# Moving eight modulation chunks within the RWKV stage of a two-block transformer kernel

## The chip, the cores and the metric

The kernel runs on one core of one Trainium2 chip. The metric is the device time of one execution in microseconds (us); for the kernel before it is the median of 3 runs.

## What is computed

Two transformer blocks on one sequence of 512 tokens of width 1024, in float32. The change lies in the first block, which mixes a dilated attention and an RWKV-7 recurrence, gated, and modulates its normalized inputs and its residuals by six vectors worked out from a conditioning vector `c`:

```python
ada = (c @ w_ada[l] + b_ada[l])[:, None, :]
sh1, sc1, gt1, sh2, sc2, gt2 = jnp.split(ada, 6, axis=-1)
h = rms_norm(x, norm1_w[l]) * (1.0 + sc1) + sh1
proj = h @ w_in[l]
att_in, rwkv_in, gate_in = jnp.split(proj, [ATT_IN, ATT_IN + RWKV_IN], axis=-1)
y_att = attention_mixer(att_in) @ w_att_out[l]
y_rwkv = rwkv7_mixer(rwkv_in, ...) @ w_rwkv_out[l]
g_att, g_rwkv = jnp.split(jax.nn.sigmoid(gate_in + b_gate[l]), N_BRANCHES, axis=-1)
x = x + gt1 * ((g_att * y_att + g_rwkv * y_rwkv) @ w_o[l])
h = rms_norm(x, norm2_w[l]) * (1.0 + sc2) + sh2
x = x + gt2 * conv_ffn(h, w_up[l], conv_w[l], conv_b[l], w_down[l])
```

`rwkv7_mixer` shifts its projections by one token, makes r, k and v from them and runs a state recurrence over the tokens for 16 heads. The second block (two attentions and a mixture of 32 experts) is not touched.

## The kernel before

**Products.** A float32 product is made of three fp32r ones. `raw_load` (line 216) fetches 1 MB of weights into one of two buffers tagged `raw`. `split` (225) copies them to `hi` on ACT and writes the rest, `lo`, on GpSimd and DVE in turn; each half of a raw buffer is the weights of one 128-row output tile, and there are four `hi`/`lo` pairs. `dense` (250) then runs 24 matmuls of 128x128 on 128x512 into a PSUM bank tagged `mm`, of which there are two (`MM`, 179). A raw buffer comes free when both halves are split.

**The modulation.** w_ada is read in 24 chunks of 256 columns, 1 MB each. The first 8 (sh1, sc1) are done before the first norm, and those from 16 on later, on DVE. Chunks 8 to 15 (gt1, sh2) are the generator `ada_group` (281), called for two groups of four: one step for each chunk (its load into a `raw` buffer, 8 matmuls with a 32-column stationary operand, 16 in the trace since float32 goes in two passes, into an `mm` bank, and a DVE copy or add into `rows`), and a fifth step that finishes a group (two transposes into an `mm` bank, a DVE reduction and an add). Chunks are not split; their `raw` buffer comes free when TensorE has read it. The results are first used behind the RWKV and attention stages.

**The RWKV stage** goes through four quarters of four heads (`rwkv_quarter`, 599). A quarter makes, for each of two tiles `i2`, the decay, then k, r and v in this order (s = 1, 0, 2; each a `dense` product whose bank `shift`, 509, empties with one instruction on ACT and one on DVE), then the small matmuls of the chunked recurrence, which it masks into `SA` and `SB` and sends through DRAM (`Ad`). Then DVE inverts 64 triangular 32x32 blocks in 31 steps (`Ti`, lines 721 to 729), the result goes through DRAM once more (`Td`) and comes back to two groups of 32x32 matmuls (`px`, `py`), and the recurrence runs over 8 chunks of 64 tokens, with three groups of small matmuls (`SA`, `TT`, `SB`) and copies in each. At its end the output is normalized per head.

**Fillers.** Beside this runs `fw`, a chain of the attention's q and k products (`f_qk`), its v products (`f_v`, 128x256 matmuls, three weight loads for each half) and the gates (`f_gate`), cut in steps. A quarter has a budget of 4 x nw steps; it pulls 28 of them at points of its recurrence, and `run_fill` (821) emits what is left behind the quarter. In the second and third quarters `run_fill` also takes five steps of `fa`, the chain of the two `ada_group`s, in turn with the fillers.

**Order.** The program is written through a tile framework: emission gives each instruction its rank, and a planner that knows what waits for what puts instructions on the engines' queues, by rank among those that it holds to be ready; buffers are handed out the same way. An engine then runs its queue in order. All weight loads and all stores go through SP's queue.

Of the kernel before, what the change touches and what calls it, by code (L numbers as in the profile page):

```python
# [161 lines left out]
def body(tc, I, O):  # L162
# [4 lines left out]
    with es:  # L167
# [8 lines left out]
        def G(tag="a"):  # L176
            return pp.tile([128, 512], F32, tag=tag, bufs=3, name=tag)

        def MM():
            return pp.tile([128, 512], F32, tag="mm", bufs=2, name="mm")  # L180

        def mm(out, l, r, start=True, stop=True):
            return nc.tensor.matmul(out, l, r, start=start, stop=stop, skip_group_check=True)  # L183
# [7 lines left out]
        def V(n, j=None, w=1):  # L191
            o, m = PVO[n]
            return pv[:, o:o + m] if j is None else pv[:, o + j:o + j + w]
# [52 lines left out]
        def pull(g, n):  # L246
            for _ in islice(g, n):
                pass

        def dense(acc, w, xs, late=False):  # L250
            hi, lo = w
            n = len(xs)
            for k, (xh, xl) in enumerate(xs):
                mm(acc, hi[:, k], xh, start=(k == 0), stop=False)
                mm(acc, hi[:, k], xl, start=False, stop=False)
                if not late:
                    mm(acc, lo[:, k], xh, start=False, stop=(k == n - 1))
            for k, (xh, _) in enumerate(xs if late else ()):
                mm(acc, lo[:, k], xh, start=False, stop=(k == n - 1))
# [21 lines left out]
        def ada_group(chs, pool=None, bufs=RAWB):  # L281


            rows = adp.tile([128, 256], F32, tag="rows", bufs=1, name="rows")
            for m, ch in enumerate(chs):
                raw = raw_load(I['wada'][ch], pool, bufs).rearrange("p (k c) -> p k c", k=8)
                acc = MM()
                for k in range(8):
                    j = k % 4
                    mm(acc[32 * j:32 * j + 32, 0:256], c32[:, k, 3 - m:35 - m], raw[:, k], start=(k < 4), stop=(k >= 4))  # L290
                if m == 0:
                    nc.vector.tensor_copy(rows, acc[:, 0:256])
                else:
                    nc.vector.tensor_add(rows, acc[:, 0:256], rows)
                yield
            n = len(chs)
            acc = MM()
            for s in range(2):
                nc.tensor.transpose(acc[:, 128 * s:128 * s + 128], rows[:, 128 * s:128 * s + 128], ident)
            o = 2 * chs[0]  # L300
            a = ada[0][:, o:o + 2 * n]
            nc.vector.tensor_reduce(a.rearrange("p (m s) -> p m s", s=2), acc[:, 0:256].rearrange("p (s j m) -> p m s j", s=2, j=4)[:, :n], axis=mybir.AxisListType.X, op=OP.add)
            nc.vector.tensor_add(a, a, V('bada', o, 2 * n))
            yield
# [204 lines left out]
        def shift(acc, m, mu, om, dst):  # L509
            nc.scalar.activation(dst[:m], acc[:m], AF.Copy, scale=om[:m])  # L510
            nc.vector.scalar_tensor_tensor(dst[:m, 1:512], acc[:m, 0:511], mu[:m], dst[:m, 1:512], op0=OP.mult, op1=OP.add)
# [36 lines left out]
        def f_qk(hg):  # L548
            for ch in range(6):
                gr, s = ch // 2, ch % 2  # L550
                for t, w in enumerate(wstream(I['wqk'][6 * hg + ch], 8)):
                    acc = MM()
                    yield from dense_g(acc, w, H)
                    o = rp.tile([128, 512], F32, tag="stg", bufs=2, name="stg")
                    if s == 0:
                        ov = o.rearrange("p (b r i) -> p b r i", b=4, r=4)
                        nc.scalar.activation(ov, acc.rearrange("p (b i r) -> p b r i", b=4, r=4), AF.Copy, scale=-0.125)
                    elif gr == 0:
                        nc.scalar.copy(o, acc)
                    else:  # L560
                        nc.scalar.copy(o.rearrange("p (r j) -> p r j", r=4), acc.rearrange("p (j r) -> p r j", r=4))
                    nc.sync.dma_start(qk_d[12 * hg + 4 * gr + 2 * s + t], o)
                    yield
# [25 lines left out]
        def f_gate(j0, j1):  # L589
            for j in range(j0, j1):  # L590
                for t, w in enumerate(wstream(I['wg'][j], 8)):
                    acc = MM()
                    yield from dense_g(acc, w, H)
                    o = gpool[0].tile([128, 512], F32, tag="stg", bufs=2, name="stg")
                    nc.scalar.activation(o, acc, AF.Tanh, scale=0.5, bias=bgh[:, 8 * t + j:8 * t + j + 1])
                    nc.sync.dma_start(gt_d[2 * j + t], o)
                    yield

        def rwkv_quarter(q, fw):
            T = lambda shape, tag, bufs=1, dt=F32: (rpa if tag in EARLY else rp).tile(list(shape), dt, tag=tag, bufs=bufs, name=tag)  # L600
            w2q = T([65, 256], "w2q")
            nc.sync.dma_start(w2q, I['w2a'][:, 256 * q:256 * q + 256])
# [15 lines left out]
            for i2 in range(2):  # L618
# [16 lines left out]
                for s in (1, 0, 2):  # L635
                    if early_rkv:
                        acc = early_rkv.pop(0)
                    else:
                        acc = MM()
                        dense(acc, next(rkv_it), H)  # L640
                    d = T([128, 512], "rkv"[s], 2 if s < 2 else 1)
                    shift(acc, 128, V('mu', 8 * s + i), omu[:, 8 * s + i:8 * s + i + 1], d)
                    z[s] = d
                    if s == 1:
                        ksq = T([128, 512], "tmp", 2)
                        nc.scalar.activation(ksq, d, AF.Square, scale=V('kk', i))
                        km2 = T([128, 512], "km2")
                        nc.scalar.activation(km2, ta, AF.Identity, scale=V('ka', i), bias=ka2[:, i:i + 1])
                        nc.gpsimd.tensor_mul(km2, km2, d)
                        BKf = T([128, 8, 2, 64], "BKf")  # L650
                        nc.gpsimd.tensor_mul(BKf[:, :, 1], c8(km2), Dh)
                    elif s == 0:
                        sps = G()
                        for t in range(4):
                            mm(sps[:, 2 * t:2 * t + 2], ksq[:, 128 * t:128 * t + 128], hs2)
                        rn = T([128, 8], "rn")
                        nc.vector.tensor_scalar(rn, sps[:, 0:8], 1e-24, None, op0=OP.max)
                        nc.scalar.activation(rn, rn, AF.Sqrt)
                        nc.vector.reciprocal(rn, rn)
                        AR = T([128, 8, 2, 64], "AR", 2)  # L660
                        nc.gpsimd.tensor_mul(AR[:, :, 1], c8(d), Dp)
                        prod = T([128, 512], "tmp", 2)
                        nc.vector.scalar_tensor_tensor(prod, d, rkh[:, i:i + 1], km2, op0=OP.mult, op1=OP.mult)
# [157 lines left out]
        def run_fill(*gens):  # L821
            gens = list(gens)
            while gens:
                for g in list(gens):
                    try:
                        next(g)
                    except StopIteration:
                        gens.remove(g)

        fa = chain(*[ada_group(range(o, o + 4)) for o in range(8, 16, 4)])  # L830
        fw = chain(f_qk(0), f_v(0), f_qk(1), f_v(1), f_gate(0, 8))
        for q, (nw, na) in enumerate(((11, 0), (14, 5), (14, 5), (10, 0))):
            fq = islice(fw, 4 * nw)
            rwkv_quarter(q, fq)
            run_fill(fq, islice(fa, na))
        ra_.close()

        yas = ExitStack()
# [162 lines left out]
        fa = ada_cols(fp, [(0, 16, 4)], after, lag=0)  # L1001
# [35 lines left out]
        fa = ada_cols(fp, [(0, 20, 4), (1, 0, 24)], [h2i])  # L1037
# [486 lines left out]
        m2, i2, oh2 = first_max(e2, 8, "y")  # L1524
# [100 lines left out]
        q = R([128, 4], "q")  # L1625
# [216 lines left out]
```

## Time and profile before

| | |
|---|---|
| median of 3 runs | 2034.93 us (2030.18 to 2035.95) |
| the profiled execution | 2040.78 us, span 2039.0 us |
| TensorE matmul busy | 1932.9 us (95%) |
| DVE, ACT, GpSimd busy | 1146.4, 728.3, 436.8 us |
| mean granted TensorE clock | 0.966 of full speed |
| last stores of the four RWKV quarters (`yrw_d`) | issued at 229, 374, 559 and 736 us |

The profile is of one execution. Its times are in microseconds from the span's start. PE is TensorE, POOL is GpSimd; PEclk is the granted TensorE clock as a share of full speed, which is 2.4 GHz, and 0.50 is 1.2 GHz. A busy TensorE is one with matmuls in it; at half clock the same matmuls take twice as long and count as busy all the time.

### The profile page before, as it was taken

To read this page: it belongs to the slowest core of one execution; us is meant where nothing else is said; L and a number is where in the kernel's file an instruction comes from. 1 tells how busy PE (TensorE), PEld (TensorE's weight loads), DVE (VectorE), ACT (ScalarE), POOL (GpSimd) and SP (SyncE) were. 2 spreads that over 40 slices of the span, in tenths; PEclk is the share of its full clock that TensorE was granted. 3 is DMA by queue.
4 is the path that set the end of the run, shared out by engine and by line. 5 is a ranking of instruction groups with operands and counts; after the bars stand their busy time and mean duration, and the time that the engine had idled before them with its cause. 6 is when DMAs were issued, how large, how long until landed. Compare 5 with 4: busy or idle time off the path is not lost. (4 is left out here: it accounts for less than half of the span.)

```text
span 2039.0 us, 28480 instructions
## 1 busy us (share of the span) xinstructions
PE 1932.9 (95%) x11085; PEld 1442.3 (71%) x11085; DVE 1146.4 (56%) x2232; ACT 728.3 (36%) x1261; POOL 436.8 (21%) x273
## 2 busy tenths in 40 slices
PE   7999999999999899999999989999999999599997
PEld 4788787787888767777887767777779667444553
DVE  4573573463437354557898873174430562467776
ACT  3533423342343243324333332354332452322222
POOL 1421311220232111131322322221111131122221
PEclk9999999997999999999999999999999899799998
DMA  7233244324234254244655544222233341699994
GB/s 298 78 105 104 80 120 146 117 95 122 92 104 166 81 199 163 95 166 145 199 194 181 181 160 147 92 90 82 89 114 104 98 181 40 241 421 424 424 423 195
DMA packets 100048, 334.11 MB, mean 164 GB/s; under 512 B 30212, under 2 KB 35080, under 8 KB 76360
## 3 DMA queue, kind: packets, MB, share of 16 engines
q1 hardware_dynamic: 97608, 323.89, 44.7%
q0 software_dynamic: 2304, 8.39, 1.1%
q8 instruction: 88, 1.44, 0.3%
q14 instruction: 48, 0.39, 0.1%
HBM read 304.98 MB, written 27.26 MB: 163 GB/s over the span
## 5 line engine op out<-in xcount | busy, mean ns | idle before, releaser
L231 POOL TENSOR_TENSOR lo<-raw,hi 128x1024 fp32r<-128x1024 f32 (+1 forms) x108 | 261.1, 2417 | 904.9 <-ACT hi L228 803.3
L228 ACT CAST hi<-raw 128x1024 fp32r<-128x1024 f32 (+1 forms) x215 | 222.3, 1038 | 368.5 <-PE mm L183 303.0
L183 PE MATMUL mm<-hl,hi 128*128 128x512 f32 x1008 | 333.3, 405 | 0.3 <-ACT stv L584 0.3
L183 PE MATMUL mm<-h,hi 128*128 128x512 f32 x784 | 248.3, 396 | 8.1 <-DVE u L1054 6.0
L231 DVE TENSOR_TENSOR lo<-raw,hi 128x1024 fp32r<-128x1024 f32 (+1 forms) x107 | 140.5, 1313 | 197.9 <-ACT hi L228 196.6
L183 PEld LDWEIGHTS mm<-hl,hi 128*128 128x128 f32 x1008 | 189.6, 191 | 42.1 <-issue 6.3
L183 PE MATMUL mm<-hl,lo 128*128 128x512 f32 x504 | 202.1, 401 | 0.0
L183 PEld LDWEIGHTS mm<-h,hi 128*128 128x128 f32 x784 | 146.5, 189 | 45.4 <-issue 12.3
L356 DVE SCALAR_TENSOR_TENSOR asum<-araw,cv,asum 128x256 f32<-128x256 f32 x224 | 151.5, 680 | 25.7 <-DMA araw<-in_wada 20.7
L183 PE MATMUL mm<-h,lo 128*128 128x512 f32 x392 | 153.9, 393 | 0.0
L183 PE MATMUL mm<-fm,hi 128*128 128x512 f32 x352 | 111.4, 397 | 6.1 <-ACT fm L1058 6.1
L183 PE MATMUL b<-h,hi 128*128 128x512 f32 x368 | 115.8, 392 | 0.0
L183 PE MATMUL mm<-gu,XT 128*64 128x512 f32 x512 | 113.2, 595 | 0.0
L183 PEld LDWEIGHTS mm<-hl,lo 128*128 128x128 f32 x504 | 96.0, 190 | 20.3 <-issue 2.2
L183 PEld LDWEIGHTS mm<-gu,XT 128*64 128x64 f32 x512 | 36.8, 138 | 73.0 <-issue 63.5
L183 PEld LDWEIGHTS mm<-h,lo 128*128 128x128 f32 x392 | 74.2, 189 | 15.8 <-issue 0.2
L183 PEld LDWEIGHTS mm<-fm,hi 128*128 128x128 f32 x352 | 66.7, 191 | 22.1 <-ACT fm L1058 6.5
L183 PEld LDWEIGHTS b<-h,hi 128*128 128x128 f32 x368 | 69.7, 190 | 14.7 <-issue 0.2
L183 PE MATMUL b<-h,lo 128*128 128x512 f32 x184 | 72.2, 392 | 0.0
L183 PE MATMUL mm<-fm,lo 128*128 128x512 f32 x176 | 69.2, 393 | 0.0
L893 ACT ACTIVATE sc<-sc,st 128x512 f32<-128x512 f32 (+3 forms) x96 | 56.3, 588 | 26.6 <-DVE st L891 22.3
L183 PE MATMUL mm<-hi,hl 128*128 128x256 f32 x384 | 57.6, 296 | 2.8 <-ACT stv L584 2.8
(522 smaller groups left out, 3554.1 us busy)
## 6 DMA issues: line engine op xcount, KB each, us to landing
gu<-in_wgu SPq DMA_DIRECT2D x32, 2048.0 KB, 15.0
araw<-in_wada SPq DMA_DIRECT2D x128, 256.0 KB, 3.3
dn<-in_wde SPq DMA_DIRECT2D x32, 1024.0 KB, 14.8
raw<-in_wup SPq DMA_DIRECT2D x22, 1024.0 KB, 4.8
raw<-in_wada SPq DMA_DIRECT2D x16, 1024.0 KB, 5.9
raw<-in_wg SPq DMA_DIRECT2D x16, 1024.0 KB, 5.0
raw<-in_wrkv SPq DMA_DIRECT2D x12, 1024.0 KB, 5.1
raw<-in_wqk SPq DMA_DIRECT2D x12, 1024.0 KB, 4.9
```

Of the source, the lines that this page charges most:

```text
L183: return nc.tensor.matmul(out, l, r, start=start, stop=stop, skip_group_check=True)
L228: nc.scalar.copy(hi[:, :n], src)
L231: eng.tensor_sub(lo[:, :n], src, hi[:, :n])
L356: nc.vector.scalar_tensor_tensor(a, raw[:, k], c, a, op0=OP.mult, op1=OP.add)
L893: nc.scalar.activation(sc[:, :W], sc[:, :W], AF.Exp, scale=-1.0, bias=st[:, 0:1], accum_out=st[:, 1:2])
```

## The change

The five steps of `fa` that the second and third quarters take are no longer emitted by `run_fill` behind the quarter. `rwkv_quarter` gets their number `na`, and pulls one step right behind a product and ahead of that product's `shift`: behind r and v of the first tile and behind k, r and v of the second. The first and fourth quarters have `na` = 0 and pull none. Nothing is added to the computation and nothing is left out.

```diff
-        def rwkv_quarter(q, fw):
+        def rwkv_quarter(q, fw, na):
...
                     else:
                         acc = MM()
                         dense(acc, next(rkv_it), H)
+                    pull(fa, na and (1 if i2 or s != 1 else 0))
                     d = T([128, 512], "rkv"[s], 2 if s < 2 else 1)
                     shift(acc, 128, V('mu', 8 * s + i), omu[:, 8 * s + i:8 * s + i + 1], d)
...
         for q, (nw, na) in enumerate(((11, 0), (14, 5), (14, 5), (10, 0))):
             fq = islice(fw, 4 * nw)
-            rwkv_quarter(q, fq)
-            run_fill(fq, islice(fa, na))
+            rwkv_quarter(q, fq, na)
+            run_fill(fq)
```

## Rows read from the trace of the kernel before

**Rows 1.** The page: granted clock in 40 slices of the span, tenths

```profile
PEclk9999999997999999999999999999999899799998
```

**Rows 2.** Stretches: length, busy us (x instructions) of PE, PEld, DVE, ACT, POOL; PEclk; DMA share; GB/s

```profile
380.00:434.00 54.00, 53.30 (x306) 42.74 (x305) 25.94 (x47) 22.81 (x32) 17.73 (x10) 1.00 0.26 87
434.00:474.00 40.00, 37.83 (x220) 33.33 (x219) 31.24 (x71) 11.39 (x18) 4.83 (x2) 1.00 0.39 129
474.00:516.00 42.00, 40.44 (x315) 31.52 (x315) 7.92 (x21) 10.16 (x20) 0.00 (x0) 0.64 0.46 136
560.00:580.00 20.00, 20.00 (x90) 16.57 (x89) 2.51 (x3) 7.93 (x10) 7.37 (x4) 1.00 0.47 156
```

**Rows 3.** Stretches, same columns: low clock in each of the four quarters

```profile
168.00:175.00 7.00, 7.00 (x79) 6.65 (x76) 0.04 (x1) 2.43 (x5) 0.00 (x0) 0.51 0.08 29
308.00:311.50 3.50, 3.50 (x14) 2.53 (x9) 0.58 (x2) 0.00 (x0) 0.00 (x0) 0.51 0.61 241
482.00:489.00 7.00, 7.00 (x54) 6.76 (x51) 1.58 (x4) 2.40 (x3) 0.00 (x0) 0.51 0.49 161
489.00:492.40 3.40, 3.40 (x71) 2.95 (x69) 0.69 (x1) 2.05 (x4) 0.00 (x0) 1.00 0.08 27
492.40:516.20 23.80, 23.80 (x107) 17.28 (x104) 4.59 (x13) 5.51 (x12) 0.00 (x0) 0.50 0.39 135
670.00:676.70 6.70, 6.15 (x70) 5.61 (x71) 1.69 (x4) 1.15 (x2) 0.00 (x0) 0.50 0.93 259
```

**Rows 4.** Order of time, PE, third quarter: start, length, line, operation, operands, [wait]

```profile
473.24 1.69 PE L183 MATMUL mm<-hi,hl 128*128 128x256 f32 x12 [2.17 <-ACT stv L584]
474.86 1.07 PE L183 MATMUL mm<-raw,c 128*32 128x256 f32 x16
...
490.29 2.21 PE L183 MATMUL b<-TT,tmp 32*32 32x32 f32 x64
...
500.89 1.92 PE L183 MATMUL mm<-raw,c 128*32 128x256 f32 x10
...
513.50 1.20 PE L183 MATMUL mm<-hi,hl 128*128 128x256 f32 x4
```

**Rows 5.** Order of time, PE, second quarter

```profile
300.83 1.07 PE L183 MATMUL mm<-raw,c 128*32 128x256 f32 x16
...
308.30 1.22 PE L183 MATMUL mm<-hl,hi 128*128 128x512 f32 x2
```

**Rows 6.** Order of time, SP's DMA issues, third quarter

```profile
453.68 0.33 SPq L222 DMA_DIRECT2D raw<-in_wada  x1
...
480.61 0.85 SPq L222 DMA_DIRECT2D raw<-in_wada  x1
491.29 0.32 SPq L586 DMA_DIRECT2D v_d<-stv  x1
491.70 0.38 SPq L222 DMA_DIRECT2D raw<-in_wada  x1
505.77 0.33 SPq L222 DMA_DIRECT2D raw<-in_wv  x1
```

**Rows 7.** Order of time, ACT and DVE: the shifts of one k and one r

```profile
386.87 0.69 ACT L510 ACTIVATE k<-mm,dv 128x512 f32<-128x512 f32 x1 [4.08 <-PE mm L183]
...
387.59 0.75 DVE L511 SCALAR_TENSOR_TENSOR k<-mm,pv,k 128x511 f32<-128x511 f32 x1 [9.52 <-ACT k L510]
...
419.46 0.68 ACT L510 ACTIVATE r<-mm,dv 128x512 f32<-128x512 f32 x1
...
420.94 0.74 DVE L511 SCALAR_TENSOR_TENSOR r<-mm,pv,r 128x511 f32<-128x511 f32 x1
```

**Rows 8.** Tile `raw`, 250 to 560 us: xcount, ns min/median/max; landing

```profile
L228 ACT CAST hi<-raw x33: 1031/1048/1069, 252.1 to 559.1; 128x1024 fp32r<-128x1024 f32 x33
L231 POOL TENSOR_TENSOR lo<-raw,hi x16: 2351/2392/2916, 253.3 to 548.3; 128x1024 fp32r<-128x1024 f32 x16
...
DMA to landing us min/median/max: 4.7/5.0/6.4
```

**Rows 9.** Order of time, PE, fourth quarter: return of the inverse

```profile
670.55 3.62 PE L183 MATMUL b<-inv,SA 32*32 32x32 f32 x64 [5.54 <-DMA inv<-Td]
```

## The prediction

> **What bounds the kernel now.** I read the clock line of the page first, then stretches of the two quarters that the change touches, then the instructions of TensorE and the issues of SP in them.
>
> The clock line [rows 1] has slices below full speed in several places; each slice is 51 us. Cut finer, the RWKV stage shows where: [rows 2, 3]. TensorE is busy 53.30 of 54 us in the third quarter's r, k and v products, and 40.44 of 42 us from 474 to 516 us. So the stage is bound by TensorE's work and by the clock it is granted, not by a transfer. In all four quarters the clock drops to 1.2 GHz (0.50 of full speed) around the 32x32 matmuls that follow the triangular inverse: for 7 us in the first, 3.5 in the second, 7 in the third and 6.7 in the fourth [rows 3]. In the third quarter alone it comes back for 3.4 us and drops a second time, for 23.8 us, with TensorE busy 23.80 of 23.80 us. At half speed that costs 23.8 x 0.5 = 11.9 us; the ordinary drop costs 3.4 us or less.
>
> Why there? Ahead of the second drop stand the second group of 32x32 matmuls (490.29 us); in the drop stand recurrence steps of 64 and 128 columns and chunk matmuls on a 32-column stationary operand, with no dense product; it ends where full 128x128 weight products appear again (513.50 us) [rows 4]. SP shows why no product was there: after 453.68 us the loads of weights into the two `raw` buffers are four chunks of w_ada (the second of them, not shown, at 466.89 us). The third goes out at 480.61; the fourth only at 491.70, behind a store of `stv` at 491.29 that waited; the next filler weights leave at 505.77 [rows 6]. A chunk keeps its buffer until TensorE has read it, while filler weights keep theirs only until split. So for 25 us both buffers serve chunks and TensorE gets none of the work that would hold its clock up. The second quarter has chunks in the same place but went on with dense work behind the first small group (308.30 us) [rows 5], and its drop lasted 3.5 us.
>
> **The order is not that of the code.** The chunks are emitted behind the whole quarter, yet they run before and inside its recurrence (300.83 and 500.89 us) [rows 4, 5]: emission gives a rank, and a planner puts what is ready into gaps. The change raises the rank of ten steps; I expect their loads and matmuls to move up to the products, since nothing else holds them.
>
> **Part by part.** Nothing is added or removed: eight chunk loads of 1 MB, 128 chunk matmuls (a chunk of 16 takes 1.07 us at full clock [rows 5]), eight DVE copies or adds and two finishing steps move; in each quarter 4 x 1.07 = 4.3 us of TensorE work moves up, in the third from between 475 and 512 us to the products. That work costs the same in either place; what can differ is this:
>
> 1. *Third quarter, second drop.* With the chunks gone, the two buffers refill with the f_v and gate weights 25 us sooner, and the recurrence is filled with full-width products, as in the first and fourth quarters, which have no chunks and no second drop [rows 3]. Gain between 11.9 us (no second drop) and 8.5 us (a second drop as long as an ordinary one: 11.9 - 3.4). I take 10.2, the middle. What is late next is the round trip of the inverse through DRAM in the fourth quarter, 5.54 us of idle TensorE [rows 9]; its chain starts from that quarter's own products, so it moves up along with them and does not eat the gain.
> 2. *Second quarter, its one drop.* It lasts 3.5 us now; without chunks it may be like the others, 7: cost 0 to 1.7, I take 0.85.
> 3. *PSUM.* Products and chunks share two `mm` banks. Now a product is 24 x 20.00 / 90 = 5.3 us [rows 2], and its bank is emptied meanwhile by ACT and DVE. With a chunk between two products, the next one needs the bank of the last after 1.07 us. The shift of r ran from 419.46 (ACT) to 420.94 + 0.74 = 421.68 us (DVE): 2.2 us [rows 7], so TensorE could wait 1.1 us there; that of k took 1.5 us (386.87 to 388.34), which leaves 0.4. In a quarter three products stand so: 1.1 + 0.4 + 0.4 = 1.9, twice 3.8 us at most. At least 0: the small matmuls that stand behind r are ready and can be put between. I take 1.0, nearer to zero, because of them. The chunk's DVE copy also ranks ahead of the shift's second half, but the shift is ready first; DVE is busy 25.94 of 54 us there [rows 2], so I cost its eight extra operations at nothing. If the copy did go first, r's or v's shift would be late by about 1 us a time; only the inverse's chain waits for it, beside which TensorE has 37.83 us of fillers from 434 to 474 us [rows 2].
> 4. *Buffers and SP.* The loads now rank A (k, r), chunk, B (v, k), chunk, chunk, C (r, v), chunk, then fillers. C waits until TensorE has read the second chunk. From there to C's use lie one product (5.3), the third chunk (1.07) and about a third of the small matmuls of the stretch: 53.30 - 7 x 5.3 = 16, a third is 5; in all 11.4 us. C needs 5.0 (landing) + 1.05 (hi) + 2.4 (lo) = 8.4 us [rows 8]. It fits with 3 us to spare. The fourth chunk has 5.3 us (a product) for 5.0: it may be late by 1 us. Behind these waiting loads on SP stand the stores of `SA`, on which the inverse waits, and the fillers' loads. Cost 0 to 1 a quarter, 0 to 2 in all; I take 0.5.
> 5. *What the chunks hid.* In the third quarter two chunks, at 474.86 us and 477.48, run right behind a wait of 2.17 us for f_v's copy [rows 4]; in the second one runs at 300.83, while the inverse's result is on its way [rows 5]. Without them TensorE may idle 3 x 1.07 = 3.2 us more; nothing, if fillers stand in their place. I take 1.0.
>
> Sum: -10.2 + 0.85 + 1.0 + 0.5 + 1.0 = -6.85 us. Best end -11.9; worst end -8.5 + 1.7 + 3.8 + 2 + 3.2 = +2.2. The profiled execution took 2040.78 us (span 2039.0), so it would come to 2033.9. The median of the shown runs lies 5.85 us lower, so a timed run may hold less of the second drop than the profiled one; I put the whole sum on the median all the same: 2034.93 - 6.85 = 2028.1, with 2023.0 to 2037.1 from its ends. The measurement tells about 0.3% from no change, 6.1 us.
>
> A page weighed against this: in these rows the clock drops at 492.4 us although TensorE was busy 3.40 of 3.40 us before [rows 3]. The Trainium skill, "TensorE: Matmul & The Clock Gate", section "Why this matters for your kernels", puts a drop down to idle gaps between bursts of matmuls. By it the second drop would come from waiting, which the change does not shorten, and the sum would lose its first term; the row speaks against it. Rival B is what that would come to here.
>
> **Rivals.**
>
> *A. Only half is won.* The 32x32 matmuls stay where they are, and the recurrence is still half narrow work; the clock may stay down for half as long, or the timed runs have the long drop only about every second time (their spread is 2030.18 to 2035.95, and the profiled one lies above all of them). For it: that spread. Against: the two quarters without chunks. 11.9 / 2 = 5.95 gained, 0.85 + 1.0 + 0.5 + 1.0 = 3.35 paid: 2032.3.
>
> *B. The clock follows TensorE's waiting, not its mix.* From 434 to 474 us TensorE is idle 40 - 37.83 = 2.2 us, and 1.6 more to 516 [rows 2]; nothing of this goes, the long drop stays, and the 3.35 is paid: 2038.3. Also what comes out if the planner leaves the chunks about where they are (then without the 3.35: 2034.9).
>
> *C. Slower: the loads get stuck.* Mechanism: SP is in order, and a load that waits for a chunk to be read holds up whatever stands behind it. For it: the fourth chunk's load left 11 us behind the third's, held by a store that waited [rows 6]. Place: C, in the second and third quarters. It decides once C leaves more than 3 us late (point 4). At 9 us late, TensorE waits 6 us a quarter before r; a wait like that is followed by a drop worth 3.4, as in the fourth quarter (5.54 us idle, then 6.7 us at half speed [rows 3, 9]). Twice 9.4 = 18.8, with 3.35, less 10.2: +12, 2046.9. Against: TensorE is busy 53.30 of 54 us in the products' stretch, so no load is late there now [rows 2].
>
> **How the numbers follow.** Forecast 0.48, A 0.24, B 0.10, C 0.18. A and B lie within 0.3% of 2034.93 (2028.8 to 2041.0), so faster 0.48, same 0.34, slower 0.18. The range takes in the forecast's ends, A and B, and leaves C out: 2022 to 2040.
>
> **What would show it.** Right: chunk matmuls between products of r, k and v in the second and third quarters; no chunk load on SP between the third inverse and its recurrence; fillers in the gaps of the recurrence there; granted clock at half for about 7 us a quarter, none of 24. Wrong in point 3 or 4: TensorE waiting for the shift of k, r or v, or for `hi` or `lo` of in_wrkv, by more than 1 us a time. Wrong in point 1: a half-speed stretch of over 10 us behind 480 us although fillers run in it. The prediction fails as a whole if the long drop stays, or if the products wait for weights.

## The result, and the profile after

The change made the kernel slower: 2085.55 us (median of 6 runs, 2077.07 to 2097.07) against 2034.3 us for the kernel before (6 runs, 2028.25 to 2045.42), a ratio of 1.0243 with a 95% interval of 1.0202 to 1.0285. That is +51 us where the prediction had -7, and above the upper end of its range. The profiled execution took 2082.37 us, 41.6 more than that of before.

First the page of after: the span, busy time of TensorE, and the granted clock in 40 slices.

```profile
span 2080.6 us, 28478 instructions
PE 1949.7 (94%) x11085; PEld 1455.6 (70%) x11085; DVE 1157.9 (56%) x2232; ACT 732.5 (35%) x1263; POOL 437.4 (21%) x273
PEclk9999888999799999998999999999999999799999
```

The instructions are the same, yet TensorE is busy 16.8 us longer (1949.7 against 1932.9), which is the same matmuls at a lower clock, and idle 24.8 us longer (2080.6 - 1949.7 = 130.9 against 2039.0 - 1932.9 = 106.1). In the clock line, slices 5 to 7 (208 to 364 us, nearly all in the second quarter) read 8 where [rows 1] has 9. The 7 of slice 10 there, the long drop of the third quarter, is gone, and slice 11, also in the third quarter here, reads 7 instead.

To place it, cut the stage where each quarter issues the last store of its output. This gives quarter lengths that can be compared between kernels; the first quarter ends at 229 to 233 us in all of them. Stretches of the second and third quarter follow, columns as in [rows 2], first the kernel before, then after:

```profile
229.40:373.60 144.20, 140.47 (x1030) 115.05 (x1029) 82.03 (x164) 51.67 (x88) 27.34 (x16) 0.99 0.37 116
373.60:559.10 185.50, 179.00 (x1150) 149.15 (x1149) 88.56 (x170) 61.02 (x99) 33.55 (x20) 0.92 0.33 107
```

```profile
231.20:402.90 171.70, 160.00 (x1063) 133.39 (x1063) 86.02 (x164) 53.99 (x88) 29.58 (x17) 0.90 0.33 106
402.90:604.40 201.50, 182.25 (x1150) 150.72 (x1149) 95.96 (x172) 66.48 (x105) 34.75 (x20) 0.90 0.30 96
604.40:783.10 178.70, 173.10 (x1067) 139.36 (x1065) 88.59 (x175) 68.33 (x101) 37.59 (x19) 0.96 0.37 120
```

The second quarter is 27.5 us longer (8.0 us more idle, 19.5 more busy, at a clock of 0.90 instead of 0.99), the third 16.0 longer; the fourth is 178.7 against 177.4, and the rest of the program is 5 us shorter. The third quarter of before holds the long drop of [rows 3] here; in two further executions without it (experiments 9 and 10) it takes 173.4 us, and the third quarter of after is 28 us longer than that. So the loss sits in the two quarters that the change touches, and the question is which wait made it. The waits of SP's queue from 150 to 290 us name it (engine and line, who released it: total us, times, longest); before, then after:

```profile
SPq L222 <- DVE lo L231: 30.7, 5, 14.3
SPq L222 <- POOL X L760: 12.8, 1, 12.8
SPq L222 <- DVE mn L805: 6.9, 1, 6.9
SPq L222 <- POOL lo L231: 1.1, 1, 1.1
```

```profile
SPq L222 <- PE mm L183: 36.3, 4, 24.4
SPq L222 <- DVE lo L231: 20.6, 5, 6.8
```

The four rows of before are all that its loads (L222) wait for: no load in this stretch waits for TensorE. After, four do, for 36.3 us. In order of time, the issues of loads on SP (start, length, line, operation, operands), before and then after:

```profile
150.79 0.33 SPq L222 DMA_DIRECT2D raw<-in_wrkv  x1
163.88 0.41 SPq L222 DMA_DIRECT2D raw<-in_wrkv  x1
187.21 0.33 SPq L222 DMA_DIRECT2D raw<-in_wrkv  x1
```

```profile
151.56 0.33 SPq L222 DMA_DIRECT2D raw<-in_wrkv  x1
164.67 0.40 SPq L222 DMA_DIRECT2D raw<-in_wada  x1
215.16 0.33 SPq L222 DMA_DIRECT2D raw<-in_wrkv  x1
224.78 0.33 SPq L222 DMA_DIRECT2D raw<-in_wada  x1
239.84 0.33 SPq L222 DMA_DIRECT2D raw<-in_wada  x1
255.21 0.36 SPq L222 DMA_DIRECT2D raw<-in_wrkv  x1
```

Before, the three product loads A (k, r), B (v, k), C (r, v) leave 13 and 23 us apart, the last of them 42 us ahead of the quarter's border. After, B leaves 50.5 us behind the first chunk, and C 40 us behind B. What each waits for is seen on TensorE:

```profile
214.03 1.07 PE L183 MATMUL mm<-raw,c 128*32 128x256 f32 x16
221.56 1.09 PE L812 MATMUL b<-c,Ti 128*128 128x128 f32 x4 [6.47 <-DVE Ti L807]
...
229.35 1.84 PE L183 MATMUL mm<-hl,hi 128*128 128x512 f32 x2
...
238.71 1.07 PE L183 MATMUL mm<-raw,c 128*32 128x256 f32 x16
...
254.07 1.07 PE L183 MATMUL mm<-raw,c 128*32 128x256 f32 x16
...
269.88 1.07 PE L183 MATMUL mm<-raw,c 128*32 128x256 f32 x16 [0.55 <-DMA raw<-in_wada]
...
282.02 2.80 PE L183 MATMUL a<-AR,BKf 64*128 64x128 f32 x16 [2.79 <-DVE bv L680]
```

The first chunk was loaded at 164.67 us, but stands behind r on TensorE and is read from 214.03 to 215.10; B leaves at 215.16. The v product, which needs B, starts at 229.35, and TensorE is idle 6.47 us ahead of it, where the v product stood before, waiting for the normalization of the first quarter. The third chunk is read until 255.14; C leaves at 255.21. The loads go through one buffer in turn: A, chunk, B, chunk, chunk, C, chunk. By the last shift of v, at 277.91 us, the quarter is 25 us behind another execution of the kernel before (252.70, experiment 9); the third quarter runs in the same way (B at 422.56, just behind a chunk read at 421.4).

Why one buffer, where there are two? The queue's order answers that. This is the order in which the program's instructions stand on SP and on ACT after the change (row on the engine, line, operands with buffer numbers, what is waited for):

```
SP   51 L222 DMA raw_1697<-in_wada 128x2048 [waits DVE_49,Pool_49]
SP   55 L222 DMA raw_1726<-in_wrkv 128x2048 [waits DMAHW4_49,DMAHW0_49,PE_49]
ACT  80 L228 CAST hi_1562<-raw_1560 128x1024
ACT 121 L228 CAST hi_1728<-raw_1726 128x1024
ACT 122 L228 CAST hi_1859<-raw_1726 128x1024
ACT 140 L228 CAST hi_1912<-raw_1910 128x1024
ACT 141 L228 CAST hi_1969<-raw_1910 128x1024
ACT 142 L228 CAST hi_2215<-raw_1560 128x1024
```

`raw_1560` is the sixth load of in_wqk, a filler. A load holds two output tiles; the first quarter's budget of 11 tiles ends between them. The first half is split in the first quarter (ACT row 80), the second only behind both halves of C (`raw_1910`; row 142, in the second quarter's filler turns). The trace has the three copies to `hi` in one row, behind the landing of C, so the filler holds one of the two buffers until 263 us:

```profile
260.13 2.94 ACT L228 CAST hi<-raw 128x1024 fp32r<-128x1024 f32 x3 [1.53 <-DMA raw<-in_wrkv]
```

The kernel before has the same held buffer, but its product loads wait only for splits, so one buffer was enough. The third quarter meets the same: with the second's budget of 14 the tenth load of in_wqk is left half split.

### The profile page after: what moved, and what is told of

Read it like the earlier page. It is cut to its first block, busy times and chain, and to the rows that moved or that the text cites. A ratio compares the mean times of both kernels' runs of the same rounds, so it can differ in the third digit from the quotient of the medians.

```text
span 2080.6 us, 28478 instructions
## 1 busy us (share of the span) xinstructions
PE 1949.7 (94%) x11085; PEld 1455.6 (70%) x11085; DVE 1157.9 (56%) x2232; ACT 732.5 (35%) x1263; POOL 437.4 (21%) x273
## 5 line engine op out<-in xcount | busy, mean ns | idle before, releaser
L183 PE MATMUL mm<-hl,hi 128*128 128x512 f32 x1008 | 344.0, 417 | 6.3 <-ACT stv L584 4.2
L183 PEld LDWEIGHTS mm<-hl,hi 128*128 128x128 f32 x1008 | 194.9, 197 | 52.7 <-issue 7.2
L356 DVE SCALAR_TENSOR_TENSOR asum<-araw,cv,asum 128x256 f32<-128x256 f32 x224 | 154.3, 692 | 23.8 <-DMA araw<-in_wada 19.3
```

The costliest lines, as they stand in the source:

```text
L356: nc.vector.scalar_tensor_tensor(a, raw[:, k], c, a, op0=OP.mult, op1=OP.add)
```

## The experiments

The theories: **H**, the held buffer: product loads and chunk loads share one buffer, and a chunk gives it back only when TensorE has read it. **P**, the place of the chunks on TensorE, DVE and the two banks costs the time, whatever the loads do.

**1 and 2. A budget of whole loads** (12 tiles in the first quarter, so that no load is left half split at the ends of the first two quarters), in the kernel after and in the kernel before.

```diff
-        for q, (nw, na) in enumerate(((11, 0), (14, 5), (14, 5), (10, 0))):
+        for q, (nw, na) in enumerate(((12, 0), (14, 5), (14, 5), (10, 0))):
```

> The changed kernel with the first quarter's filler budget raised from 11 to 12, so that no quarter ends with a weight load of which only one half is split. Theory H (a half-split filler load holds one of the two raw buffers through the products of r, k and v, so that product loads and chunk loads go through one buffer and each product load waits until TensorE has read a chunk): most of the 51 us between the two kernels comes back, 2034 to 2052 us, the third load of in_wrkv in the second quarter leaves without waiting for TensorE, and TensorE's waits for bv, tmp, rn, hi and lo in the products go. Rival P (the place of the chunk between a product and its shift: PSUM banks, DVE copies): stays at 2078 to 2095 us.

> The kernel before with the same budget of 12, as the control for after_even. Theory H: the kernel before loses little by the held buffer, since its product loads follow each other and are early enough: 2024 to 2038 us. Rival P says nothing of it: 2034 us within 6.

Measured: 2053.64 us with the change (4 runs; ratio to the kernel before 1.0085, 1.005 to 1.0119) and 2051.28 without (4 runs; 1.0071, 1.0029 to 1.0113). With whole loads the change costs 2.4 us, not 51. From the end of the first quarter to that of the fourth it takes 518.2 us against 515.6 (552.0 for after, 507.1 for before), and TensorE's waits for `bv`, `tmp`, `rn`, `hi` and `lo` are gone. H holds for the greater part, with two misses: the second and third quarters together are still 11.2 us longer than without the change (334.3 against 323.1), which the fourth makes up for in this pair, and C still leaves at 234.40 us, just behind the second chunk, which is read from 233.27 to 234.34, where the expectation had it leave without that wait. Both medians also lie above the ranges expected. The new budget has a price of its own, 0.7%, which I had not expected: in the profiled execution of before with it, the fourth quarter has 23.9 us at half clock at 672 us and 30.7 at 724, and is 192.5 us long against 177.4.

**3 and 4. No chunk loads.** The chunk matmuls stay where they are, but read a resident tile, so that gt1 and sh2 are not computed from w_ada.

```diff
-                raw = raw_load(I['wada'][ch], pool, bufs).rearrange("p (k c) -> p k c", k=8)
...
-                    mm(..., c32[:, k, 3 - m:35 - m], raw[:, k], start=(k < 4), stop=(k >= 4))
+                    mm(..., c32[:, k, 3 - m:35 - m], pv[:, 0:256], start=(k < 4), stop=(k >= 4))
```

> The changed kernel with the eight chunk loads left out: the chunk matmuls read a resident table of parameters in place of w_ada, so that gt1 and sh2 are not computed from w_ada. Matmuls, PSUM banks, DVE operations and their places stay. Theory H: 2026 to 2046 us, no product load waits for a chunk. Rival P: 2075 to 2090 us, since all that it names is still there.

> The kernel before with the eight chunk loads left out in the same way (gt1 and sh2 are not computed from w_ada). It takes the prediction's first term by itself: if chunk loads in the two raw buffers are what keeps dense work out of the third quarter's recurrence, the second clock drop there is gone or as long as an ordinary one, and the time is 2021 to 2030 us. If the drop comes from waits and narrow matmuls whoever holds the buffers, it stays at 15 us or more and the time is 2030 to 2037 us.

Measured: 2140.9 us with the change and 2144.9 without (4 runs each; ratios 1.0529 and 1.0542 to the kernel before). Both miss every absolute figure expected: the program behind the RWKV stage takes 1404 to 1412 us instead of 1302, and TensorE has 11343 matmuls instead of 11085. I put this down to other gt1 and sh2, with which the second block would send tokens to other experts; it is not shown. Within the stage they can be read: from the first quarter's end to the fourth's it takes 493.1 us with the change and 505.7 without it, and the second quarter takes 143.5 and 144.8. The 12.6 us between them are clock: the execution without the change is at half clock 27 us longer in these quarters, which costs it some 13 us. So the two are level. With the loads gone, moving the matmuls, the copies and the bank turns costs some 1 us, against 51. P falls as the cause of the loss. What it names is there in small: with the change TensorE waits twice, 2.4 us in all, for the copy `rows` from 200 to 300 us. Experiment 4 was also to test the prediction's first term: without chunk loads the third quarter has drops of 6.8 and 3.4 us and no long one. That decides nothing, since experiments 9 and 10 have no long one either, with the loads in place.

**5 and 6. The held load cut in two.** The two loads of in_wqk that stand across a border are made as two half loads, so that the first half's buffer comes free in its own quarter. Budgets stay.

```diff
-                for t, w in enumerate(wstream(I['wqk'][6 * hg + ch], 8)):
+                c_ = I['wqk'][6 * hg + ch]
+                ws = chain(wstream(c_[:, 0:1], 8), wstream(c_[:, 1:2], 8)) if 6 * hg + ch in (5, 9) else wstream(c_, 8)
+                for t, w in enumerate(ws):
```

> The changed kernel with its budgets as they are; two of the twelve in_wqk loads, those of which one half would be left over at the end of the first and of the second quarter, are made in two halves, so that the left-over half holds no raw buffer. Theory H (the held buffer): in the products the second load of in_wrkv waits for a split and no longer for a chunk to be read; 2034 to 2055 us, the end of the third quarter at 555 to 570 us of the span instead of 604. Rival P (place of the chunks, PSUM banks, DVE): 2078 to 2095 us.

> The kernel before with the same two loads in halves, as control. Theory H: 2028 to 2040 us, since its product loads were in time anyway. If freeing the buffer is worth something by itself (earlier filler weights), 2020 to 2030 us.

Measured: 2045.89 us with the change (10 runs; 1.0038, 1.0008 to 1.0067) and 2040.79 without (10 runs; 1.0015, 0.9975 to 1.0056); the kernel before had 2039.67 beside them. The first lies in the range of H, the second 0.8 us above it. Of the 51 us, some 45 are gone by the medians (5.1 are left). The issues on SP show B leaving at once, ahead of need:

```profile
164.41 0.45 SPq L222 DMA_DIRECT2D raw<-in_wada  x1
164.95 0.40 SPq L222 DMA_DIRECT2D raw<-in_wrkv  x1
190.07 0.33 SPq L222 DMA_DIRECT2D raw<-in_wada  x1
216.37 0.33 SPq L222 DMA_DIRECT2D raw<-in_wada  x1
229.85 0.37 SPq L222 DMA_DIRECT2D raw<-in_wrkv  x1
```

B at 164.95, half a us behind the first chunk, where after had 215.16. C still leaves late, at 229.85, because the second chunk must be read first; the waits of SP in this stretch keep that part:

```profile
SPq L222 <- PE mm L183: 31.6, 2, 25.4
```

The second quarter is 159.7 us long in this execution (144.4 for the same edit without the change), and the median is 5.1 us above that of the same edit in the kernel before. Their intervals overlap, so this rest is a size, not a proof. Within the three quarters more is left: they take 514.3 us in the profiled execution against 497.7 without the change, and the rest of the program is 13.7 us shorter in it. What makes it stays open: TensorE waits for no product weights in this quarter, but for DVE, as its waits from 210 to 300 us say (who waits, for whom: total us, times, longest).

```profile
PE a L183 <- DVE SB L695: 2.3, 1, 2.3
PE a L183 <- DVE AR L680: 1.5, 1, 1.5
```

One more thing is seen here: the first chunk's copy went ahead of r's shift on DVE, and the next product's matmuls waited for it.

```profile
217.11 0.72 PE L183 MATMUL mm<-hl,hi 128*128 128x512 f32 x2 [0.80 <-DVE rows L292]
```

**7 and 8. All five steps behind the last product of the quarter**, with the in_wqk loads as they were and with the two cut in halves. The chunks then load behind C, and no product load can stand behind a chunk.

```diff
-                    pull(fa, na and (1 if i2 or s != 1 else 0))
+                    pull(fa, na if i2 and s == 2 else 0)
```

> The changed kernel with all five steps of a quarter pulled behind its last product (v of the second tile) instead of one behind each. The held buffer stays. Theory H: product loads rank ahead of the chunks and leave as in the kernel before, so the waits in the products are gone; the chunk loads now go one by one through the free buffer ahead of the filler loads, and cost something there: 2036 to 2060 us. Rival P: with the five steps in a row in place of between products, PSUM waits remain once a chunk: 2050 to 2080 us.

> Both edits that took the loss away in one kernel: the five steps of a quarter behind its last product, and the two in_wqk loads that would leave a half over made in halves. Theory H: product loads and the free buffer as in before_halves, chunk loads in two buffers: 2025 to 2040 us, second and third quarter together 5 to 12 us shorter than in the kernel before (329.7 us). If the gain of the third quarter is lost again to the clock further on, 0.995 to 1.005 of the kernel before.

Measured: 2032.72 us (10 runs; 0.998, 0.9944 to 1.0016) and, with cut loads as well, 2037.17 (12 runs; 1.0007, 0.9976 to 1.0039). Both are level with the kernel before. The held buffer is still there in the first of them and costs nothing that the median shows, less than the 2036 to 2060 us expected: it hurts when chunks must pass through the other buffer ahead of product weights. In the second, the second and third quarters together take 327.4 us, 2.3 less than in the first profiled execution of before and not the 5 to 12 expected; against the executions of experiments 9 and 10 (317.7) they are longer. The product loads leave as before, and the chunks behind them:

```profile
152.43 0.33 SPq L222 DMA_DIRECT2D raw<-in_wrkv  x1
165.52 0.41 SPq L222 DMA_DIRECT2D raw<-in_wrkv  x1
190.31 0.33 SPq L222 DMA_DIRECT2D raw<-in_wrkv  x1
218.04 7.40 SPq L222 DMA_DIRECT2D raw<-in_wada  x2
254.52 2.45 SPq L222 DMA_DIRECT2D raw<-in_wada  x2
```

No version beats the kernel before by what can be measured.

**9 and 10. The kernel before again**, two more profiled executions, unchanged but for empty lines at the end of the file, to see whether the long second drop of the third quarter belongs to the kernel.

> The kernel before, profiled once more. The prediction's first term takes the 23.8 us at half clock in the third quarter as a property of the kernel: then it is there again, 17 us or longer behind the second group of 32x32 matmuls. If it is chance (rival A), it is 7 us or absent in this run or the next.

> The kernel before, profiled a third time; expected as for before_b.

Measured: 2029.28 and 2039.62 us. Neither has the long drop: each shows two spells of 3.4 us at half clock in the third quarter, which takes 173.4 us instead of 185.5. From the first of them, the third quarter and the very stretch of the long drop in [rows 3], columns as there:

```profile
375.60:549.00 173.40, 168.54 (x1150) 141.22 (x1149) 89.10 (x171) 61.06 (x99) 33.52 (x20) 0.98 0.35 114
...
492.40:516.20 23.80, 23.71 (x177) 19.38 (x176) 10.03 (x24) 9.98 (x20) 2.81 (x2) 0.93 0.49 174
```

From 492.4 us on the clock is 0.93 here and was 0.50 there. The same instructions stand in the same order, the 32x32 matmuls and then a chunk:

```profile
488.96 2.21 PE L183 MATMUL b<-TT,tmp 32*32 32x32 f32 x64
...
497.22 1.05 PE L183 MATMUL mm<-raw,c 128*32 128x256 f32 x10
```

Ten matmuls of the chunk took 1.05 us here and 1.92 in [rows 4]. So the drop of 23.8 us was in one of three executions and does not belong to the kernel. The execution at 2039.62 is about as long as the first without having it: its program behind the stage takes 1311.6 us instead of 1302.5. What one execution loses at one place, another loses elsewhere.

**Clock and waits apart.** Since such spells come and go, the three quarters (first quarter's end to fourth's) compare better with half of their time at half clock taken off, an estimate of their length at full clock from the clock of each trace. It gives 486.2 to 486.6 us for the three executions of before and 507.5 for after, so some 21 us of the loss are waits and the rest of it is clock. TensorE's idle time agrees, 36.6 us in after against 14.8 in experiment 9. At half clock are 89 us in after, and 41, 17 and 17 in those of before. With the change against without it, whole loads have 487.2 and 484.7, no chunk loads 488.0 and 486.9, and cut loads 497.3 and 487.5; experiments 7 and 8 have 489.7 and 489.0. These are single executions, but they rank the edits as H does, and they show that cutting the held load leaves some 10 us where whole loads leave 2.5.

## Why the prediction was wrong, point by point

**What bounds the kernel: right, and its use wrong.** TensorE and its clock bound the stage, and no transfer was late [rows 2]. But that said how far ahead the loads of before ran (C left 42 us ahead of the border), and the prediction never read how many of the two buffers they ran ahead with.

**Point 4, buffers and SP: the step that failed.** It ranked the loads rightly (A, chunk, B, chunk, chunk, C) and knew that a chunk keeps its buffer until it is read. It then put A in one buffer and the chunk in the other and let only C wait, with 3 us to spare: 0.5 us. There was one buffer, so B waited for the first chunk to be read behind r: 50.5 us between their issues, 14 us from B's issue to v's first matmul. The term came to some +45 us instead of +0.5, by what goes away with the held buffer alone: experiments 5 and 6 show that with a free second buffer B leaves half a us behind the chunk, and the change costs 5.1. In that case C does leave 7 us behind the shift of v (222.90), as point 4 ordered it, and TensorE has no wait for its `hi` or `lo`: for C, point 4's reckoning would have stood, had there been two buffers.

**Rival C** had the kind of mechanism (a load that waits for a chunk to be read holds up what is behind it) and the right sign, at 2046.9 us with a chance of 0.18. It put the place at C and the cause in SP's order, and counted 6 us of waiting a quarter and 3.4 of clock. Measured were 8.0 us more idle and 19.5 us more busy time in the second quarter and, against experiment 9, which has no long drop, 14.4 and 13.7 in the third: more idle time than it said, and with it a far larger loss of clock. In after a spell of 17.1 us at half clock begins at 217.5 us, inside the 6.47 us of idle TensorE; most of it lies ahead of the border at 231.2. In the second quarter itself spells of 6.8 us follow the idle times of 1.96 and 0.83 us before 259 and of 2.79 us before 282.02 (stretches, columns as in [rows 2]):

```profile
217.50:234.60 17.10, 13.04 (x28) 7.86 (x28) 3.99 (x5) 6.60 (x9) 6.15 (x5) 0.50 0.39 146
258.46:265.30 6.84, 5.56 (x24) 3.99 (x25) 4.51 (x4) 3.08 (x4) 3.48 (x2) 0.50 0.12 49
282.35:289.20 6.85, 6.85 (x30) 5.84 (x29) 3.65 (x9) 1.16 (x2) 0.00 (x0) 0.50 0.16 32
```

The first of these is what the Trainium skill, "TensorE: Matmul & The Clock Gate", section "Why this matters for your kernels", says of idle gaps between bursts of matmuls; here the trace agrees, with 6.47 us. The prediction weighed that rule against a drop with TensorE busy 3.40 of 3.40 us [rows 3], found that the row spoke against it, and kept it as rival B at 0.10, for waits that are there already. For waits that the change itself makes only rival C priced it, at 3.4 us a quarter, where the second quarter alone has 34 us at half clock, against 3.4 before: 15 us more.

**Point 1, the gain of 10.2 us: there was none to win in two executions out of three.** Two further executions of before do not have the long drop. The median of the runs lay 5.85 us below the profiled execution, which the prediction noted and then set aside; rival A had said that the runs may have the drop only now and then. Nor does such a spell need chunks: in after, one as long comes at 528.1 us, with no chunk in it.

```profile
528.10:552.00 23.90, 22.48 (x187) 19.51 (x186) 3.00 (x8) 7.81 (x15) 0.00 (x0) 0.50 0.24 72
```

There TensorE runs the 32x32 matmuls and the fillers' 128x256 products. What starts the long spell in one execution and not in the next stays open.

**Point 2, the second quarter's drop,** is not settled: with all chunks moved and no product load late, that quarter is at half clock for 6.8 us in the execution of experiment 7 and 10.2 in that of experiment 8, against 3.4 in the three of before, which is the sign predicted; in that of experiment 3 it has no drop at all.

**Point 3, PSUM:** right in kind, and rather short. Waits for the shift or for the copy `rows` do come between products: 1.3 us over the two quarters in experiment 5, its first in the order that the point called unlikely, 2.9 in experiment 3 and 5.4 in experiment 1, where 1.0 was taken and 3.8 was the most. In after itself it is 0.2.

**Point 5, what the chunks hid:** nothing was seen of it. Without any wait for loads the three quarters are level (experiments 3 and 4, 488.0 and 486.9 us with the clock taken out).

**What would show it.** The prediction said that it fails as a whole if the products wait for weights. They did, and SP's waits for TensorE, 36.3 us, were the first row to show it.

## What to carry to other kernels

Before a load is moved ahead of another in a ring of buffers, count the buffers that are free at that point, not those that exist: look for a load whose use is cut in two by a budget, and at what each buffer's release waits for (here a split early on, or a read by TensorE 50 us later). A load that is released late belongs behind those that are needed soon, as experiment 7 has it, or gets a buffer of its own (not tried here). A clock drop in one execution is priced only when a second execution has it in the same place.

## What the runs showed of the hardware that I had not expected

The same program in three profiled executions had 23.8 us at half clock in one place or none there, with the same instructions in the same order, and the runs of the kernel before in one session went from 2023.63 to 2051.78 us. The granted clock goes with it: of the six runs of after, the shortest, 2077.07 us, had a mean clock of 0.957 and the longest, 2097.07, one of 0.948. And a wait can cost more than its length: 6.47 us of idle TensorE were followed by 17.1 us at half clock, of which 13.04 us were busy, which by itself is some 6.5 us more.
